# Block norms of a two-layer decoder trunk: from one root per token, spread by a diagonal product, to a ones product and roots on all partitions

## The chip, the cores and the metric

The kernel runs on one core of one Trainium2 chip. The metric is device time in microseconds for one execution of the whole program. A profiled execution leaves a trace besides; its span runs from the first to the last instruction that the profiler recorded.

## What is computed

The reference is a trunk of two layers over 512 tokens plus 16 meta tokens (528 columns here), with a model width of 1024. Everything is float32. Each layer is a feed-forward block, a token mixer and a second feed-forward block. The mixer of layer 0 is gated linear attention (GLA), that of layer 1 sliding-window attention over keys and values that are made once, after layer 0. Each of the six sub-layers has a norm on its input and a norm on its output:

```python
def rmsnorm(x, g):
    xf = x.astype(jnp.float32)
    y = xf * lax.rsqrt(jnp.mean(xf * xf, axis=-1, keepdims=True) + EPS)
    return (y * g.astype(jnp.float32)).astype(x.dtype)

h = h + 0.5 * rmsnorm(swiglu(rmsnorm(h, g[0]), w_ffn_in[layer, 0], w_ffn_out[layer, 0]), g[1])
...
h = h + rmsnorm(mix, g[3])
h = h + 0.5 * rmsnorm(swiglu(rmsnorm(h, g[4]), w_ffn_in[layer, 1], w_ffn_out[layer, 1]), g[5])
```

The mean runs over the 1024 features of a token. GLA has one more norm per head, over 256 features.

## The kernel before, in words

**Layout.** Features lie on the 128 partitions and tokens along the columns: H (the residual stream) and Y (a block's output) are tiles of 128 x 8 x 528. A norm therefore needs a sum across partitions, and its result, one number per token, is needed on every partition. Tokens come in two groups, columns 0 to 271 and 272 to 527 in layer 0 (`L0`), 16 to 271 and 272 to 527 in layer 1 (`L1`).

**Products.** TensorE (PE) multiplies in a split form. Each weight tile and each operand is kept as a high part, rounded by ScalarE (ACT), and a low part, the remainder that VectorE (DVE) makes by a subtraction; three products make one (`mm3`). Weights come by DMA into raw tiles and are split by `split_part` (L228, L229) or, for Strassen products, by `split_pair` (L248, L249; POOL issues the adding DMAs of L254). All products have the line of the helper `mm`, L164, so they are told apart by the names of their tiles.

**Norms.** `square_into` (L402, L405, L406) squares on ACT and sums six of eight feature tiles on GpSimd (POOL); first and last tile keep a buffer of their own (`acc`, six buffers), so a norm's sums are two tiles of 128 x n. A post-norm is `Residual.run`: `rstd` makes the roots, then for each of eight feature tiles DVE multiplies Y by them (L467) and adds to H (L468), `Operand.build` makes the next block's operand x from H (ACT L428 and DVE L429), and `sumsq` squares it for the pre-norm. The last post-norm, `Residual.store`, multiplies two feature tiles at a time (L482), adds (L483, partly on POOL) and sends the output (L485). A pre-norm is `Operand.factors`: x goes into its products without the root, and the root row R scales the products when they leave PSUM (L643, L647, L843 and others), so those evacuations wait for the job `rjob` of their group.

**rstd.** For c tokens at a time (128, or 68 for 272 columns) a product with a single column of ones puts the sums of c tokens into one column of the PSUM tile `st` (L357). The result has tokens on partitions: 128 x 2 or 68 x 4 numbers. A magic constant and two refining steps give the inverse root, ten small operations on DVE (post-norms and the two norms at the opening) or eleven on POOL behind one on ACT (L366). Then a diagonal matrix `dg` (L386) times ones, the tile `r`, spreads the roots over all partitions (L394). For post-norms r stays in PSUM and is read there; for pre-norms ACT copies it into R (L445).

**Order of the work.** All engines take their instructions in program order, and that order is planned when the program is written. `Flow` keeps a clock that PE's products advance, and every generator yields planned microseconds: `DCHAIN` (3.0) between st and r where the roots are made on DVE, `CHAIN` (5) where POOL makes them, 1.0 after each feature tile. A step that has come due is put into the queues at PE's next product. PSUM has eight banks (`ps`). At a block's end, `out_steps` finishes the first group's tiles, spawns its `Residual.run`, and multiplies the second group's tiles meanwhile; `x_first` then multiplies the next block's first four weight tiles for the first group, while the second group's post-norm runs, and then for the second group.

Of the kernel before, what the change touches and what calls it, by code (L numbers as in the profile page):

```python
# [11 lines left out]
I32 = mybir.dt.int32  # L12
AF = mybir.ActivationFunctionType
ALU = mybir.AluOpType
AX = mybir.AxisListType

P = 128
D = 1024
# [9 lines left out]
RSQRT_MAGIC = float(0x5F3759DF)  # L28
# [9 lines left out]
CHAINS = 2  # L38

CHAIN = 5  # L40
DCHAIN = 3.0
FACT = 1.5
START = 1.0
SECOND = 6.0
# [81 lines left out]
def trunk_kernel(ctx: ExitStack, tc, a, out):  # L126
    nc = tc.nc
    pe, act, dve, pool, sp = nc.tensor, nc.scalar, nc.vector, nc.gpsimd, nc.sync
# [11 lines left out]
    ident = cp.tile([P, P], F32, name="ident")  # L140
    hident = cp.tile([P, P], F32, name="hident")
    ones = cp.tile([P, P], F32, name="ones")
    eps = cp.tile([P, 1], F32, name="eps")
    zeros = cp.tile([P, P], F32R, name="zeros")

    def ps(name):
        return pp.tile([P, 512], F32, tag="ps", name=name)

    def pair_tile(name, dt=F32R):
        return hp.tile([P, 2, TOK], dt, tag="pair", name=name)  # L150
# [5 lines left out]
    def flat(t):  # L156
        return t.rearrange("p a t -> p (a t)")

    def gain(layer, i, k):
        c = V_GAIN + layer * 48 + i * 8 + k  # L160
        return vec[:, c : c + 1]

    def mm(o, lhs, rhs, start=True, stop=True, onto=False):
        inst = pe.matmul(o, lhs, rhs, start=start, stop=stop, skip_group_check=onto)  # L164
        n = 1
        for d in rhs.shape[1:]:
            n *= d
        flow.clock += n / 2400 if rhs.dtype == F32R else max(n / 600, 0.12)
        return inst
# [178 lines left out]
        mm3s([(o, w)], j, x, g, start, stop)  # L348


    def rstd(sq, n, dim, half, name, eng=pool):
        c = 128 if n % 128 == 0 else n // 4
        nch = n // c
        st = ps(f"st_{name}")
        for j in range(nch):
            for i, t in enumerate(sq):
                mm(st[:c, j : j + 1], t[:, j * c : (j + 1) * c], ones[:, 0:1], i == 0, i == len(sq) - 1)  # L357
        av = sm.tile([P, 4], F32, tag="av", name=f"av_{name}")
        yv = sm.tile([P, 4], F32, tag="yv", name=f"yv_{name}")
        zv = sm.tile([P, 4], F32, tag="zv", name=f"zv_{name}")  # L360
        wv = sm.tile([P, 4], F32, tag="wv", name=f"wv_{name}")
        aa, yy, zz, ww = av[:c, :nch], yv[:c, :nch], zv[:c, :nch], wv[:c, :nch]
        if eng is dve:
            dve.tensor_scalar(aa, st[:c, :nch], 1.0 / dim, 1e-6, op0=ALU.mult, op1=ALU.add)
        else:
            act.activation(aa, st[:c, :nch], AF.Identity, scale=1.0 / dim, bias=eps[:c])  # L366
        eng.tensor_scalar(yy.bitcast(I32), aa.bitcast(I32), -0.5, RSQRT_MAGIC, op0=ALU.mult, op1=ALU.add)

        eng.tensor_tensor(zz, yy, yy, op=ALU.mult)
        eng.tensor_tensor(zz, zz, aa, op=ALU.mult)  # L370
        eng.tensor_scalar(ww, zz, 0.375, -1.25, op0=ALU.mult, op1=ALU.add)
        eng.tensor_tensor(ww, ww, zz, op=ALU.mult)
        if eng is dve:
            dve.scalar_tensor_tensor(yy, ww, 1.875, yy, op0=ALU.add, op1=ALU.mult)
            dve.tensor_tensor(zz, yy, yy, op=ALU.mult)
            dve.scalar_tensor_tensor(zz, zz, -0.5, aa, op0=ALU.mult, op1=ALU.mult)
            dve.scalar_tensor_tensor(yy, zz, 1.5, yy, op0=ALU.add, op1=ALU.mult)
        else:
            pool.tensor_scalar(ww, ww, 1.875, None, op0=ALU.add)
            pool.tensor_tensor(yy, yy, ww, op=ALU.mult)  # L380
            pool.tensor_tensor(zz, yy, yy, op=ALU.mult)
            pool.tensor_tensor(zz, zz, aa, op=ALU.mult)
            pool.tensor_scalar(zz, zz, -0.5, 1.5, op0=ALU.mult, op1=ALU.add)
            pool.tensor_tensor(yy, yy, zz, op=ALU.mult)
        dg = sm.tile([P, 272], F32, tag="dg", name=f"dg_{name}", bufs=2)
        eng.tensor_tensor(  # L386
            dg[:c, :n].rearrange("p (j c) -> p j c", c=c),
            (hident if half else ident)[:c, :c].unsqueeze(1).to_broadcast([c, nch, c]),
            yy.unsqueeze(2).to_broadcast([c, nch, c]),
            op=ALU.mult,  # L390
        )
        yield DCHAIN if eng is dve else CHAIN
        r = ps(f"r_{name}")
        mm(r[:, :n], ones[:c, :], dg[:c, :n])  # L394
        return r


    def square_into(sums, src, i, count, name):
# [14 lines left out]
    class Operand:  # L413


        def __init__(self, name, gv, groups, rt=None):
            self.name, self.gv, self.groups, self.tiles = name, gv, groups, [None] * KD
            self.ready = set()
            self.rt = rt
            self.rjob = [None] * len(groups)  # L420
            self.accs = [[] for _ in groups]
# [14 lines left out]
            o, n = self.groups[gi]  # L436
            square_into(self.accs[gi], H[:, k, o : o + n], k, KD, f"{self.name}_{o}_{k}")

        def factors(self, gi, eng=pool):
            if self.rt is None:  # L440
                self.rt = sm.tile([P, TOK], F32, tag="R", name=f"R_{self.name}", bufs=2)
            o, n = self.groups[gi]
            yield FACT
            r = yield from rstd(self.accs[gi], n, D, False, f"{self.name}_{o}", eng)
            act.activation(self.rt[:, o : o + n], r[:, :n], AF.Copy)  # L445

        def need(self, gi, k):
            flow.until(lambda: (gi, k) in self.ready)
# [1 line left out]

    class Residual:
        def __init__(self, name, layer, i, half, nxt=None):
            self.name, self.half, self.nxt = name, half, nxt
            self.gain = lambda m: gain(layer, i, m)

        def run(self, gi, g, sums):
            o, n = g
            nxt = self.nxt
            yield 1.8
            r = yield from rstd(sums, n, D, self.half, f"post_{self.name}{gi}", dve)  # L460
            if nxt is None:
                yield from self.store(gi, g, r)
                return
            for k in range(KD):
                h, y = H[:, k, o : o + n], Y[:, k, o : o + n]
                t = r[:, 256 : 256 + n] if n <= 256 else ps(f"t_{self.name}{gi}{k}")[:, :n]
                dve.tensor_tensor(t, y, r[:, :n], op=ALU.mult)  # L467
                dve.tensor_tensor(h, t, h, op=ALU.add)  # L468
                nxt.build(gi, k)
                nxt.sumsq(gi, k)  # L470
                yield 1.0
            nxt.rjob[gi] = flow.spawn(nxt.factors(gi))

        def store(self, gi, g, r):
            o, n = g
            rb = r[:, :n].unsqueeze(1).to_broadcast([P, 2, n])
            for k in range(0, KD, 2):
                h, y = H[:, k : k + 2, o : o + n], Y[:, k : k + 2, o : o + n]
                last = gi == 1 and k < 4
                t = flat(pair_tile(f"t_{self.name}{k}", F32))[:, :512] if last else ps(f"t_{self.name}{gi}{k}")  # L480
                t = t.rearrange("p (k n) -> p k n", n=n)
                dve.tensor_tensor(t, y, rb, op=ALU.mult)  # L482
                (pool if last else dve).tensor_tensor(h, t, h, op=ALU.add)  # L483
                for j in (k, k + 1):
                    sp.dma_start(out[j, :, o - META : o - META + n], H[:, j, o : o + n])  # L485
                yield 1.0
# [330 lines left out]
    def gla(x, finish):  # L817
        set_ahead(10)
        with tc.tile_pool(name="gp", bufs=1) as gp:
# [61 lines left out]
            def core(h, before):  # L881
# [73 lines left out]
                s = flat(pair_tile(f"st{h}", F32))[:, :1024].rearrange("p (b v) -> p b v", v=256)  # L955
# [12 lines left out]
                for i in range(2):  # L968
                    vs = slice(i * P, (i + 1) * P)
                    p = ps(f"po{h}_{i}")  # L970
                    for b in range(4):
                        o = p[:, b * P : (b + 1) * P]
# [5 lines left out]
                yy = Y[:, 2 * h : 2 * h + 2]  # L978
                dve.tensor_copy(yy[:, :, :META], pm[:, : 2 * META].rearrange("p (i m) -> p i m", m=META))
                accs = []  # L980
# [3 lines left out]
                        square_into(accs[gi], Y[:, 2 * h + i, o : o + n], i, 2, f"go{h}_{gi}")  # L984
                yield 2.0
                def scale(gi, o, n):
                    r = yield from rstd(accs[gi], n, 256, True, f"go{h}_{gi}")
                    dve.tensor_tensor(
                        yy[:, :, o : o + n], yy[:, :, o : o + n],
                        r[:, :n].unsqueeze(1).to_broadcast([P, 2, n]), op=ALU.mult,  # L990
                    )
# [241 lines left out]
    x = Operand("l0f0", lambda k: gain(0, 0, k), L0)  # L1233
# [6 lines left out]
    def factors(gi):  # L1240
        for k in range(KD):
            x.sumsq(gi, k)
            yield 0.4
        yield START
        yield from x.factors(gi, dve)

    def second():
        for k in range(KD):
# [37 lines left out]
    nxt, fin = into("l0m", 0, 1, True, lambda k: gain(0, 2, k), L0)  # L1286
    ffn(x, L0, fin, True)
    x = nxt
    nxt, fin = into("l0f1", 0, 3, False, lambda k: gain(0, 4, k), L0)
    gla(x, fin)  # L1290
    x = nxt
    nxt, fin = into("kv", 0, 5, True, lambda k: vec[:, V_KVN + k : V_KVN + k + 1], L0)
# [3 lines left out]
    with tc.tile_pool(name="kp", bufs=1) as kp:  # L1296
        x = Operand("l1f0", lambda k: gain(1, 0, k), L1)
# [8 lines left out]
        nxt, fin = into("l1m", 1, 1, True, lambda k: gain(1, 2, k), L1)  # L1306
        ffn(x, L1W, fin)
        x = nxt
        nxt, fin = into("l1f1", 1, 3, False, lambda k: gain(1, 4, k), L1)
# [87 lines left out]
```

## Time and profile before

| | us |
|---|---|
| median of 3 runs | 1923.98 |
| lowest and highest | 1922.87, 1925.53 |
| the profiled execution | 1922.4 |
| its span | 1920.6 |
| PE busy in the span | 1885.4 |
| DVE, ACT, POOL busy | 1340.4, 993.5, 341.4 |

The profiled execution lies 1.6 us under the median. Busy times of engines overlap and don't add up. PE has two rows: PE for products and PEld for the loads of the stationary operand, which overlap with products. A row of a group gives line, engine, operation, tiles written and read, shapes, the count, busy us and the mean ns of one, and then the idle time before them with what ended it. A row in order of time begins with start and duration in us. In names such as `st_post_l0m` the last part is the block that comes next: l0f (twice: first and second feed-forward of layer 0), l0m (GLA), kv, l1f, l1m (attention), out.

### The profile page before, as it was taken

How to read it: one execution, taken by the hardware profiler on the slowest of the kernel's cores; microseconds unless marked ns; L12 is line 12 of the kernel's file. 1: busy time of each engine (PE TensorE's matmuls, PEld its weight loads, DVE VectorE, ACT ScalarE, POOL GpSimd, SP SyncE). 2: the span in 40 equal slices, each digit the busy share in tenths (PEclk: the TensorE clock that was granted, in tenths of full speed). 3: DMA queues.
4: the chain of work that ended last, by engine and by line, in shares of the span. 5: the costliest groups of instructions: out<-in, count | busy, mean ns of one | idle time of the engine just before them, and what ended most of it. 6: DMA issues, size and time to landing. Idle time of an engine off the chain costs nothing.

```text
span 1920.6 us, 37874 instructions
## 1 busy us (share of the span) xinstructions
PE 1885.4 (98%) x14522; PEld 1798.7 (94%) x14522; DVE 1340.4 (70%) x2724; ACT 993.5 (52%) x2268; POOL 341.4 (18%) x561
## 2 busy tenths in 40 slices
PE   8999999999999999999999999999998999999997
PEld 8999999999999999999999898989976898989897
DVE  7884848676364787475877775858688778758584
ACT  5662626553245556363674563636645665636363
POOL 2101010311111410101034011010351141010102
PEclk9999999999999999999999999999998999999998
DMA  5655556222113145556642356565321215565651
GB/s 180 149 154 142 153 142 171 98 78 74 38 56 111 57 121 149 149 149 149 161 159 56 96 148 157 144 159 165 111 67 34 69 50 126 148 152 157 152 144 45
DMA packets 133253, 231.29 MB, mean 120 GB/s; under 512 B 14928, under 2 KB 27728, under 8 KB 133072
## 3 DMA queue, kind: packets, MB, share of 16 engines
q1 hardware_dynamic: 112048, 190.99, 30.8%
q0 software_dynamic: 20736, 37.76, 12.6%
q8 instruction: 113, 1.85, 0.4%
q14 instruction: 68, 0.56, 0.1%
q10 hardware_dynamic: 288, 0.13, 0.0%
HBM read 226.72 MB, written 2.10 MB: 119 GB/s over the span
## 4 chain that ended last, share of the span: by engine, by line
PE 89%; DVE 6%; ACT 2%; POOL 1%; issue 1%; DMA 0%; SPq 0%; DVEq 0%; POOLq 0%; ACTq 0%
PE y L164 31%; PE a L164 21%; PE x L164 16%; PE c L164 9%; PE d L164 5%; PE o L164 1%; DVE w L229 1%; PE e L164 1%; PE po L164 1%; PE sc L164 1%; ACT w L228 1%; PE ps L164 0%; DVE x_l0f L429 0%; PE st_go L164 0%; DVE w_s L249 0%
## 5 line engine op out<-in xcount | busy, mean ns | idle before, releaser
L254 POOL DMA_DIRECT2D raw<-in_w_in x144 | 125.9, 935 | 968.2 <-DMA raw<-in_w_in 443.9
L249 DVE TENSOR_TENSOR w_s<-raw,w_s 128x512 fp32r<-128x512 f32 x288 | 194.8, 688 | 109.3 <-ACT w_s L248 107.6
L164 PE MATMUL y<-hidl0f,w 128*128 128x272 f32 (+1 forms) x2112 | 261.0, 285 | 0.0
L164 PEld LDWEIGHTS y<-hidl0f,w 128*128 128x128 f32 x2112 | 258.8, 188 | 0.2
L229 DVE TENSOR_TENSOR w<-raw,w 128x512 fp32r<-128x512 f32 x378 | 243.7, 672 | 21.0 <-ACT w L228 18.7
L164 PE MATMUL y<-hidl1f,w 128*128 128x512 f32 (+1 forms) x1344 | 249.4, 346 | 0.0
L164 PEld LDWEIGHTS y<-hidl1f,w 128*128 128x128 f32 x1344 | 212.3, 188 | 33.2 <-ACT hidl1f L410 0.5
L248 ACT ACTIVATE w_s<-raw 128x512 fp32r<-128x512 f32 x288 | 177.6, 625 | 108.8 <-DVE raw L264 69.1
L228 ACT ACTIVATE w<-raw 128x512 fp32r<-128x512 f32 x378 | 207.9, 587 | 35.0 <-PE y L164 26.9
L249 DVE TENSOR_TENSOR w<-raw,w 128x512 fp32r<-128x512 f32 x216 | 145.2, 687 | 37.6 <-ACT w L248 35.9
L164 PE MATMUL x<-x_l0m,w 128*128 128x272 f32 (+1 forms) x1200 | 158.3, 288 | 0.0
L248 ACT ACTIVATE w<-raw 128x512 fp32r<-128x512 f32 x216 | 130.4, 621 | 47.9 <-PE y L164 47.6
L164 PEld LDWEIGHTS x<-x_l0m,w 128*128 128x128 f32 x1200 | 149.4, 188 | 1.2
L590 DVE TENSOR_TENSOR Y<-y,Y 128x256 f32<-128x256 f32 (+2 forms) x176 | 82.1, 473 | 92.0 <-PE y L164 91.6
L164 PE MATMUL a<-zl0f_t,w_s 128*128 128x264 f32 x864 | 117.0, 285 | 0.0
L164 PE MATMUL a<-zl1f_t,w_s 128*128 128x256 f32 x864 | 114.2, 281 | 0.7 <-ACT c L783 0.6
L164 PEld LDWEIGHTS a<-zl0f_t,w_s 128*128 128x128 f32 x864 | 110.1, 188 | 0.0
L164 PEld LDWEIGHTS a<-zl1f_t,w_s 128*128 128x128 f32 x864 | 106.9, 188 | 1.8 <-ACT c L783 1.7
L406 POOL TENSOR_TENSOR acc_post<-acc_post,sq_post 128x256 f32<-128x256 f32 (+1 forms) x72 | 57.5, 799 | 281.2 <-ACT sq_post L405 280.8
L164 PE MATMUL x<-x_l0f,w 128*128 128x256 f32 (+1 forms) x768 | 99.6, 289 | 7.3 <-ACT w L228 5.8
L164 PEld LDWEIGHTS x<-x_l0f,w 128*128 128x128 f32 x768 | 96.3, 191 | 8.6 <-ACT w L228 5.8
L164 PE MATMUL x<-x_l1f,w 128*128 128x256 f32 (+1 forms) x576 | 92.9, 320 | 0.0
(487 smaller groups left out, 3411.0 us busy)
## 6 DMA issues: line engine op xcount, KB each, us to landing
raw<-in_w_in SPq DMA_DIRECT2D x424, 256.0 KB, 3.8
raw<-in_w_in POOLq DMA_DIRECT2D x144, 256.0 KB, 5.0
raw<-in_w_out SPq DMA_DIRECT2D x96, 256.0 KB, 3.5
raw<-in_gla_in SPq DMA_DIRECT2D x50, 256.0 KB, 3.2
raw<-in_w_last SPq DMA_DIRECT2D x48, 256.0 KB, 3.5
raw<-in_w_out SPq DMA_DIRECT2D x64, 128.0 KB, 3.0
raw<-in_gla_out SPq DMA_DIRECT2D x16, 256.0 KB, 2.8
raw<-in_w_q SPq DMA_DIRECT2D x16, 256.0 KB, 3.8
```

The lines of the kernel that those rows point to most:

```text
L164: inst = pe.matmul(o, lhs, rhs, start=start, stop=stop, skip_group_check=onto)
L228: act.activation(w[:, 0, :m], raw[:, :m], AF.Copy)
L229: dve.tensor_tensor(w[:, 1, :m], raw[:, :m], w[:, 0, :m].bitcast(F32), op=ALU.subtract)
L248: act.activation(w[:, 0, :512], src, AF.Copy)
L249: dve.tensor_tensor(w[:, 1, :512], src, w[:, 0, :512].bitcast(F32), op=ALU.subtract)
L254: pool.dma_start(dst, src, accum_op=ALU.add)
L406: pool.tensor_tensor(sums[0][:, :n], sums[0][:, :n], t[:, :n], op=ALU.add)
L590: dve.tensor_tensor(y, p[:, :n], y, op=ALU.add)
```

## The change

The norms of `Residual` and `Operand` no longer call `rstd`; it stays for GLA's head norms alone, on POOL. They call a new function, `roots`. It multiplies the two tiles of sums by the full 128 x 128 matrix of ones, which puts each token's sum on every partition (tile `st`, 128 x n in PSUM). One planned microsecond later (`SUMMED`, 1.0) it puts five operations into the queues: on ACT the table function Abs_reciprocal_sqrt and a Square of it, on DVE one Newton step in three operations. The result is written into SBUF: into the second tile of sums for a post-norm, into R for a pre-norm. There is no diagonal, no r, and no copy into R. In a post-norm with at most 256 columns the two halves of the bank `st` serve in turns as the scratch for Y times root.

```diff
-DCHAIN = 3.0
+SUMMED = 1.0
...
+    def roots(sums, n, c, name, dst=None):
+        s = ps(f"st_{name}")
+        for i, t in enumerate(sums):
+            mm(s[:, :n], ones, t[:, :n], i == 0, i == len(sums) - 1)
+        yield SUMMED
+        q, y = sums[0][:, :n], sums[1][:, :n] if dst is None else dst
+        act.activation(y, s[:, :n], AF.Abs_reciprocal_sqrt, scale=1.0 / D, bias=eps)
+        act.activation(q, y, AF.Square, scale=D ** -0.5)
+        dve.scalar_tensor_tensor(q, s[:, :n], D * 1e-6, q, op0=ALU.add, op1=ALU.mult)
+        dve.tensor_scalar(q, q, -0.5 * c, 1.5 * c, op0=ALU.mult, op1=ALU.add)
+        dve.tensor_tensor(y, q, y, op=ALU.mult)
+        return y, s
...
-        def factors(self, gi, eng=pool):
+        def factors(self, gi):
...
             yield FACT
-            r = yield from rstd(self.accs[gi], n, D, False, f"{self.name}_{o}", eng)
-            act.activation(self.rt[:, o : o + n], r[:, :n], AF.Copy)
+            yield from roots(self.accs[gi], n, 1.0, f"{self.name}_{o}", self.rt[:, o : o + n])
...
-            r = yield from rstd(sums, n, D, self.half, f"post_{self.name}{gi}", dve)
+            r, s = yield from roots(sums, n, self.c, f"post_{self.name}{gi}")
...
-                t = r[:, 256 : 256 + n] if n <= 256 else ps(f"t_{self.name}{gi}{k}")[:, :n]
-                dve.tensor_tensor(t, y, r[:, :n], op=ALU.mult)
+                c = k % 2 * 256
+                t = s[:, c : c + n] if n <= 256 else ps(f"t_{self.name}{gi}{k}")[:, :n]
+                dve.tensor_tensor(t, y, r, op=ALU.mult)
...
-            rb = r[:, :n].unsqueeze(1).to_broadcast([P, 2, n])
+            rb = r.unsqueeze(1).to_broadcast([P, 2, n])
...
-        yield from x.factors(gi, dve)
+        yield from x.factors(gi)
```

More of the change, by code (lines that the diff above doesn't have):

```diff
@@ L348, in mm3, with rstd @@
         mm3s([(o, w)], j, x, g, start, stop)
-    def rstd(sq, n, dim, half, name, eng=pool):
+    def rstd(sq, n, dim, name):
         c = 128 if n % 128 == 0 else n // 4
@@ L362, in rstd @@
         aa, yy, zz, ww = av[:c, :nch], yv[:c, :nch], zv[:c, :nch], wv[:c, :nch]
[L363 to L384, printed above, removed]
+        act.activation(aa, st[:c, :nch], AF.Identity, scale=1.0 / dim, bias=eps[:c])
@@ new lines, in rstd @@
+        pool.tensor_scalar(yy.bitcast(I32), aa.bitcast(I32), -0.5, RSQRT_MAGIC, op0=ALU.mult, op1=ALU.add)
+        pool.tensor_tensor(zz, yy, yy, op=ALU.mult)
+        pool.tensor_tensor(zz, zz, aa, op=ALU.mult)
+        pool.tensor_scalar(ww, zz, 0.375, -1.25, op0=ALU.mult, op1=ALU.add)
+        pool.tensor_tensor(ww, ww, zz, op=ALU.mult)
+        pool.tensor_scalar(ww, ww, 1.875, None, op0=ALU.add)
+        pool.tensor_tensor(yy, yy, ww, op=ALU.mult)
+        pool.tensor_tensor(zz, yy, yy, op=ALU.mult)
@@ L385, in rstd @@
+        pool.tensor_tensor(zz, zz, aa, op=ALU.mult)
+        pool.tensor_scalar(zz, zz, -0.5, 1.5, op0=ALU.mult, op1=ALU.add)
+        pool.tensor_tensor(yy, yy, zz, op=ALU.mult)
         dg = sm.tile([P, 272], F32, tag="dg", name=f"dg_{name}", bufs=2)
-        eng.tensor_tensor(
+        pool.tensor_tensor(
             dg[:c, :n].rearrange("p (j c) -> p j c", c=c),
-            (hident if half else ident)[:c, :c].unsqueeze(1).to_broadcast([c, nch, c]),
+            hident[:c, :c].unsqueeze(1).to_broadcast([c, nch, c]),
@@ L391, in rstd @@
         )
-        yield DCHAIN if eng is dve else CHAIN
+        yield CHAIN
         r = ps(f"r_{name}")
@@ L452, in __init__ @@
         def __init__(self, name, layer, i, half, nxt=None):
-            self.name, self.half, self.nxt = name, half, nxt
+            self.name, self.c, self.nxt = name, 0.5 if half else 1.0, nxt
             self.gain = lambda m: gain(layer, i, m)
@@ L986, in scale @@
                 def scale(gi, o, n):
-                    r = yield from rstd(accs[gi], n, 256, True, f"go{h}_{gi}")
+                    r = yield from rstd(accs[gi], n, 256, f"go{h}_{gi}")
                     dve.tensor_tensor(
```

## The prediction

> **What bounds the kernel now.** I read the page first, then busy time by stages, then TensorE's weight loads in order of time, then its waits. The page's first lines:
>
> ```profile
> span 1920.6 us, 37874 instructions
> PE 1885.4 (98%) x14522; PEld 1798.7 (94%) x14522; DVE 1340.4 (70%) x2724; ACT 993.5 (52%) x2268; POOL 341.4 (18%) x561
> PE 89%; DVE 6%; ACT 2%; POOL 1%; issue 1%; DMA 0%; SPq 0%; DVEq 0%; POOLq 0%; ACTq 0%
> ```
>
> TensorE (PE) is busy for 98% of the span and carries 89% of the chain that ended last. A share over the whole span can hide the stages where block norms sit, so the next view cuts those out: stage, its length, then PE, PEld, DVE, ACT, POOL busy us.
>
> ```profile
> 345.00:425.00 80.00, 80.00 (x657) 79.09 (x656) 50.01 (x127) 45.34 (x99) 26.38 (x53) 1.00 0.20 65
> 610.00:690.00 80.00, 78.77 (x653) 78.00 (x653) 56.59 (x133) 41.80 (x98) 23.83 (x45) 1.00 0.17 47
> 980.00:1060.00 80.00, 78.43 (x646) 76.97 (x645) 59.09 (x154) 41.15 (x97) 32.64 (x55) 1.00 0.21 61
> 1360.00:1430.00 70.00, 67.61 (x504) 61.85 (x502) 47.98 (x127) 33.76 (x85) 39.04 (x64) 1.00 0.13 41
> 1535.00:1595.00 60.00, 59.95 (x435) 56.22 (x434) 46.94 (x118) 35.60 (x83) 26.39 (x48) 1.00 0.21 58
> 1906.30:1920.60 14.30, 2.18 (x10) 1.32 (x9) 6.15 (x18) 0.92 (x2) 2.48 (x2) 0.65 0.22 73
> ```
>
> The first five are the boundaries between sub-layers, where a post-norm (Residual) and the next pre-norm (Operand.factors) lie. PE idles there for 0, 1.2, 1.6, 2.4 and 0.05 us, 5.2 us in all. So even there PE is the bound: an instruction taken off PE is worth its own time, and a shorter chain on another engine is worth almost nothing, except in the last line, the 14.3 us after the last block product, where PE is nearly empty and latency counts in full.
>
> **The change, part by part.** It touches 24 norms: 6 Residuals and 6 Operands with two token groups each. Seven of these groups have 272 columns (the first group of three Residuals and of four Operands), 17 have 256. The eight head norms of GLA keep rstd.
>
> *TensorE.* Before, a norm puts sums into columns (st) and later spreads the roots with one product (r). PE's weight loads around one boundary, start and length:
>
> ```profile
> 378.69 1.13 PEld L164 LDWEIGHTS st_l0m<-ones,acc_l0m 128*68 128x68 f32 x16
> 379.74 0.97 PEld L164 LDWEIGHTS st_post_l0m<-ones,acc_post 128*128 128x128 f32 x8
> 380.63 4.33 PEld L164 LDWEIGHTS x<-x_l0m,w 128*128 128x128 f32 x34
> 384.90 0.31 PEld L164 LDWEIGHTS r_post_l0m<-dg_post_l0m,ones 128*128 128x128 f32 x2
> 385.24 0.53 PEld L164 LDWEIGHTS x<-x_l0m,w 128*128 128x128 f32 x3
> 385.71 0.32 PEld L164 LDWEIGHTS r_l0m<-dg_l0m,ones 68*128 68x128 f32 x2
> 386.06 4.67 PEld L164 LDWEIGHTS x<-x_l0m,w 128*128 128x128 f32 x36
> ```
>
> The cost of a group is from its start to the next row's start. st costs 1.05 us for 272 columns (16 instructions) and 0.89 for 256 (8 instructions, a single output column each); r costs 0.35 and 0.34. An f32 product is two instructions in the trace. After, a norm is two products ones x sums, each with the stationary operand, width and type of r, so 2 x 0.34 or 2 x 0.35. Per norm of 256: 0.89 + 0.34 - 0.68 = 0.55 us less. Per norm of 272: 1.05 + 0.35 - 0.70 = 0.70 less. 17 x 0.55 + 7 x 0.70 = **14.3 us less PE work**, all in stages where PE is the bound. What is late next there are the weights and x tiles behind PE; the five stages' 5.2 us of idle PE say that both mostly keep up now.
>
> *Waits of PE.* From PE's waits (us in total, times, longest):
>
> ```profile
> PE r_post_out L164 <- DVE dg_post_out L386: 2.6, 1, 2.6
> PE st_l1m L164 <- POOL acc_l1m L406: 1.1, 1, 1.1
> PE st_l0f L164 <- ACT acc_l0f L402: 1.1, 1, 1.1
> PE r_post_kv L164 <- DVE dg_post_kv L386: 0.7, 1, 0.7
> PE st_kv L164 <- POOL acc_kv L406: 0.6, 1, 0.6
> PE r_l0f L164 <- DVE dg_l0f L386: 0.5, 1, 0.5
> PE r_kv L164 <- POOL dg_kv L386: 0.2, 1, 0.2
> PE r_l0f L164 <- POOL dg_l0f L386: 0.2, 1, 0.2
> ```
>
> The product r goes away, and with it the only place where PE waits for the roots: 0.7 + 0.5 + 0.2 + 0.2 = **1.6 us less** (the 2.6 is in the tail, below). The waits of st for its sums stay, now before the ones product; I count them unchanged.
>
> *The chain of one norm.* The post-norm of the same boundary's second group, on DVE:
>
> ```profile
> 380.84 0.16 DVE L364 TENSOR_SCALAR av_post_l0m<-st_post_l0m 128x2 f32<-128x2 f32 x1 [3.14 <-PE st_post_l0m L164]
> 382.82 0.42 DVE L386 TENSOR_TENSOR dg_post_l0m<-hident,yv_post_l0m 128x256 f32<-128x256 f32 x1
> 385.65 0.43 DVE L467 TENSOR_TENSOR r_post_l0m<-Y,r_post_l0m 128x256 f32<-128x256 f32 x1 [2.41 <-PE r_post_l0m L164]
> ```
>
> From st to the first multiply it is 385.65 - 379.74 = 5.9 us; 1.7 of them pass between the diagonal's end (383.24) and r's turn in PE's queue (384.90), an order fixed by the planner's yield. The new operations have no row of their own, so they are bounded by these:
>
> ```profile
> L867 ACT ACTIVATE az<-z,vec 128x272 f32<-128x272 f32 (+1 forms) x8 | 3.3, 488 | 4.1 <-PE z L164 4.1
> L868 DVE TENSOR_SCALAR ls<-z,vec 128x256 f32<-128x256 f32 x4 | 1.9, 478 | 0.0
> L371 DVE TENSOR_SCALAR wv_post_l1m<-zv_post_l1m 128x2 f32<-128x2 f32 x2 | 0.3, 170 | 0.1
> ```
>
> The root is an ACTIVATE from PSUM with a bias pointer, as L867: 0.49. Square: 0.41, as the first row of the three under the table loads below. The three DVE operations on 128x256 lie between 0.17 (the same kind on two columns) and 0.48; I take 0.43 for each, as the diagonal and the multiply above take 0.42 and 0.43. From r's weight load to the reader is 385.65 - 384.90 = 0.75. New chain: 0.34 + 0.75 + 0.49 + 0.41 + 3 x 0.43 + some 0.15 of handoffs = 3.4 us, 2.5 shorter. By the bounds it is 2.6 to 3.6. In these stages that buys nothing by itself; it is slack.
>
> *Load on the other engines.* DVE: 14 old chains (12 post, two at the opening) of ten small operations in 2.0 us (380.84 to 382.82) and a diagonal of 0.42, 34 us, against 24 x 1.29 = 31. POOL loses ten chains. ACT gains 24 x (0.49 + 0.41) = 22 us, less the ten small av rows and twelve R copies that go, **and table loads**.
>
> *Table loads.* All of them today, and one in order of time:
>
> ```profile
> L644 ACT ACT_TABLE_LOAD x3 | 3.8, 1283 | 0.1
> L1231 ACT ACT_TABLE_LOAD x1 | 1.3, 1283 | 1.2 <-PEq L1386 1.2
> L872 ACT ACT_TABLE_LOAD x1 | 1.3, 1283 | 0.0
> L905 ACT ACT_TABLE_LOAD x1 | 1.3, 1283 | 0.0
> L1162 ACT ACT_TABLE_LOAD x1 | 1.3, 1283 | 0.7 <-DVE nm L1158 0.7
> ```
> ```profile
> 1570.40 0.41 ACT L405 ACTIVATE sq_l1f<-H 128x256 f32<-128x256 f32 x1
> 1570.83 1.28 ACT L644 ACT_TABLE_LOAD   x1
> 1572.12 0.42 ACT L644 ACTIVATE gu<-gu 128x256 f32<-128x256 f32 x1
> ```
>
> Seven loads: Silu, Ln and Exp need theirs; Copy, Square and Identity need none. I assume the root needs a table apart from Silu's and Exp's. By the order of the code that gives, beyond the seven: opening 3, into GLA 2 (root, then Tanh again), into the second FFN 3, shared KV 2, attention 1, last FFN 3, end 1: 15 more, 15 x 1.283 = 19.2 us of ACT. If it shares Silu's table it is almost none. ACT is busy 45 of 80, 42 of 80, 41 of 80, 34 of 70 and 36 of 60 us in the five stages, so 1.3 to 3.8 us more fits. Most lie off the path of the x tiles: the root's first load comes while PE multiplies the second token group of the block before; Silu's load among the second group's x tiles is there already (1570.83); and the reloads for the second pre-norm come when all x tiles of that norm are built. Their cover is the x products that PE has queued; without it each costs 1.28.
>
> [...]
>
> *Queues.* All five operations of a norm are put into ACT's and DVE's queues 1.0 us of planned time after the products. DVE's three wait at the queue's head for ACT's two (0.9 us, 2.2 with a load). Behind them on DVE stand the block's evacuations (L590), weight splits (L229) and the multiplies of the other group; for those wait PE's banks and x tiles. The second group's x tiles are the tight spot. I charge **2 us more** over the kernel, between -3 (the shorter chain and a POOL free for the L406 sums take away idle PE) and +31 (second rival).
>
> *The tail.* From the last sum to the last multiply:
>
> ```profile
> 1907.26 0.74 PEld L164 LDWEIGHTS st_post_out<-ones,acc_post 128*128 128x128 f32 x6 [0.89 <-ACT acc_post L402]
> 1912.04 2.49 DVE L482 TENSOR_TENSOR t_out<-Y,r_post_out 128x512 f32<-128x512 f32 x4 [1.45 <-PE r_post_out L164]
> ```
>
> After: 1907.26 + 0.75 (second product) + 0.49 + 0.41 + 1.29 + 0.15 = 1910.4, no load among them, as the first group has already fetched the table. That is **1.6 us less**.
>
> **Sum.** -14.3 - 1.6 - 1.6 + 2 = -15.5. The profiled execution took 1922.4 us (span 1920.6 and 1.8 around it), so 1906.9. The median of the runs, 1923.98, is 1.6 above that execution; on its scale the forecast is 1908.
>
> **The rivals.**
> (1) *More is won.* The shorter chain and the free POOL also remove idle PE at the boundaries and the st waits of 1.1, 1.1 and 0.6: about 5 us more, with 2 us not charged, 1902. For it: the second group's x tiles start 2.5 us earlier. Against: their pace is set by DVE's work per tile, which stays.
> (2) *Slower: PE waits for x tiles because DVE stands behind ACT.* Place: the second group at each boundary. Price if nothing is hidden: 24 x 0.9 of DVE standing and 15 x 1.28 of loads, 41 us, less about 2 us of slack at each of five boundaries, 31: 1922.4 - 17.5 + 31 = 1936. It decides once about 17 of the 41 reach PE. For it: DVE is 63 to 78% busy there (50 of 80 to 47 of 60). Against: the old chain held PE back 1.7 us in its queue and the new one doesn't. [...]
> (3) *Partly hidden.* Half of the loads beside x tiles show, some 8 us: 1916.
> (4) *The ones product is no cheaper* than st and r together: then only waits and tail remain, -3.2 + 2, 1922 to 1923. The row of r, same operands and width, speaks against it.
>
> **How the numbers follow.** Forecast 0.58 (1905 to 1912), (1) 0.14, (3) 0.12, (2) 0.10, (4) 0.06. The range is 1899 to 1921. A difference of 0.2% (3.9 us) is about what a measurement can tell from none. Forecast, (1) and (3) are faster: 0.84; (4) is mostly no difference, 0.06; (2) slower, 0.10.
>
> **What would show it.** Right: PE's busy time falls by some 14 us; no rows r_post or R copies; st rows of four instructions with about 0.7 us to the next row; 22 table loads or so; t_out starts 3.1 us after the last sum. Wrong: new PE waits for x tiles or w in the five stages, ends of DVE waits on the root's line over 2 us, or s products that cost over 0.5 us each.

## The result, and the profile after

The changed kernel takes 1935.34 us (median of 6 runs, 1931.64 to 1937.82) against 1922.98 (6 runs, 1922.22 to 1925.53): ratio **1.0055, interval 1.0044 to 1.0066**, so slower by half a per cent. The forecast was 1908. The page after, the lines that answer to the three shown of before:

```profile
span 1934.6 us, 37301 instructions
PE 1883.9 (97%) x14322; PEld 1794.5 (93%) x14322; DVE 1357.9 (70%) x2642; ACT 1026.4 (53%) x2309; POOL 316.1 (16%) x441
...
PE 84%; DVE 9%; ACT 4%; issue 1%; POOL 1%; DMA 0%; SPq 0%; DVEq 0%; ACTq 0%; POOLq 0%
```

PE has 200 instructions fewer, yet is busy only 1.5 us less, and the span is 14.0 us longer. So PE's idle time grew by 15.5 us, and its remaining work became longer. DVE and ACT hold 13% of the chain that ended last, where they held 8%. The boundaries, stage by stage as before (each shifted by the time already lost, the last two 2 us longer):

```profile
345.00:425.00 80.00, 77.20 (x585) 75.14 (x584) 49.21 (x106) 46.53 (x97) 21.92 (x29) 0.96 0.15 50
615.00:695.00 80.00, 77.69 (x618) 76.17 (x618) 61.44 (x126) 49.06 (x108) 18.61 (x21) 1.00 0.16 47
985.00:1065.00 80.00, 73.54 (x577) 71.55 (x576) 59.69 (x136) 44.13 (x98) 25.96 (x31) 0.98 0.20 56
1368.00:1440.00 72.00, 67.39 (x479) 60.66 (x479) 53.45 (x125) 37.92 (x93) 35.29 (x40) 0.98 0.13 45
1548.00:1610.00 62.00, 58.45 (x401) 54.35 (x399) 50.35 (x109) 40.31 (x88) 18.97 (x23) 0.97 0.17 48
```

PE now idles 2.8, 2.3, 6.5, 4.6 and 3.6 us there, 19.7 in all where it was 5.2, and its granted clock (the third number from the end) is below 1 in four of the five. What it waits for, in the view of PE's waits (us in total, times, longest), behind a first row of 5.7 us at the opening that was there before (5.8):

```profile
PE ptm L176 <- DVE mt L1175: 5.1, 2, 2.9
PE st_kv L164 <- POOL acc_kv L411: 4.8, 2, 3.1
PE st_l1m L164 <- POOL acc_l1m L411: 3.9, 2, 2.6
PE pk L176 <- DVE f L920: 3.3, 1, 3.3
PE st_l1f L164 <- POOL acc_l1f L411: 2.0, 1, 2.0
PE st_l0m L164 <- POOL acc_l0m L411: 2.0, 1, 2.0
PE o L164 <- DVE pt L1196: 1.8, 1, 1.8
PE st_kv L164 <- ACT acc_kv L407: 1.6, 2, 1.0
```

The st rows are the ones products of pre-norms, which stand in PE's queue before their sums of squares are there. All st waits but the tail's come to 18.7 us (1.5 of them at a post-norm), against 2.8 before. That growth of 15.9 us is as large as all of PE's new idle time. The other waits change too, but nearly cancel: those for r are gone (4.2 us with the tail's), and so are those for sc in attention (6.7), while those for ptm, pk and o, steps of attention and GLA, grow by 8.2. In order of time at the boundary that the prediction showed (weight loads):

```profile
375.26 0.30 PEld L164 LDWEIGHTS st_l0m<-acc_l0m,ones 128*128 128x128 f32 x2 [2.18 <-POOL acc_l0m L411]
376.98 0.50 PEld L164 LDWEIGHTS st_l0m<-acc_l0m,ones 128*128 128x128 f32 x2 [1.42 <-ACT acc_l0m L407]
377.60 6.53 PEld L164 LDWEIGHTS x<-x_l0m,w 128*128 128x128 f32 x33
384.07 0.75 PEld L164 LDWEIGHTS st_post_l0m<-acc_post,ones 128*128 128x128 f32 x4
384.85 8.04 PEld L164 LDWEIGHTS x<-x_l0m,w 128*128 128x128 f32 x63
```

Two waits of 2.18 and 1.42 us, one for each tile of sums. Then 33 loads of x products take 6.5 us, where 63 take 8.0 a little later: 0.20 us apiece against 0.13. The clock says why:

```profile
376.00:380.00 4.00, 3.18 (x12) 2.79 (x12) 1.63 (x5) 3.28 (x8) 1.28 (x3) 0.50 0.00 0
380.00:384.00 4.00, 4.00 (x25) 4.00 (x24) 0.72 (x2) 0.00 (x0) 0.00 (x0) 0.69 0.00 0
384.00:390.00 6.00, 6.00 (x47) 5.90 (x47) 3.52 (x10) 2.34 (x6) 0.00 (x0) 1.00 0.02 4
```

From 376 to 380 PE is granted half its clock, in the next 4 us 0.69 of it: by single microseconds 0.50 from 376 to 382, 0.74 in the next, 1.00 from 383. Waits of 3.6 us by the weight loads thus cost about 6. The rows show this fall after these two waits; how long a wait brings it was not shown.

Why the sums are late is in the chain of the post-norm ahead of it. DVE and ACT for the first group before kv, from product to first multiply:

```profile
990.38 0.76 PEld L164 LDWEIGHTS st_post_kv<-acc_post,ones 128*128 128x128 f32 x4
...
991.78 1.28 ACT L395 ACT_TABLE_LOAD   x1
993.07 0.49 ACT L395 ACTIVATE acc_post<-st_post_kv,eps 128x272 f32<-128x272 f32 x1
...
993.46 0.62 ACT L228 ACTIVATE w<-raw 128x512 fp32r<-128x512 f32 x1
...
994.38 0.42 ACT L396 ACTIVATE acc_post<-acc_post 128x272 f32<-128x272 f32 x1
...
995.31 0.78 DVE L398 TENSOR_SCALAR acc_post<-acc_post 128x272 f32<-128x272 f32 x1
...
996.60 0.80 DVE L472 TENSOR_TENSOR t_kv<-Y,acc_post 128x272 f32<-128x272 f32 x2
```

That is 6.2 us from 990.38 to 996.60: the load, ACT's other work between root and Square (a weight split and a gain), and a DVE operation of 0.78. Of the six first groups four take 5.2 to 5.5 us, this one 6.2, and the one before the second feed-forward 4.1, where the load ran ahead of the product. The old chain took as long (986.93 to 993.29 in the trace of before), but the plan gave it 3.0 us and gives the new one 1.0. And many of the multiplies that follow are slower. They read two operands from SBUF now, Y and the root row; psumroot and nopool below test whether that is why. DVE's groups by form:

```profile
L472 DVE TENSOR_TENSOR st_post_l1m<-Y,acc_post 128x256 f32<-128x256 f32 x16 | 8.7, 544 | 0.2
...
L472 DVE TENSOR_TENSOR t_kv<-Y,acc_post 128x272 f32<-128x272 f32 x8 | 5.0, 638 | 0.0
```

The same multiplies took 422 and 436 ns with the root row in PSUM. Over all 80 of them DVE is busy 44.4 us instead of 34. One that is slow, beside POOL's row:

```profile
1002.14 1.71 POOL L411 TENSOR_TENSOR acc_kv<-acc_kv,sq_kv 128x272 f32<-128x272 f32 x2 [0.54 <-ACT sq_kv L410]
```
```profile
1002.19 1.03 DVE L472 TENSOR_TENSOR t_kv<-Y,acc_post 128x272 f32<-128x272 f32 x1
```

The tail shows it at its largest:

```profile
1922.10 0.30 PEld L164 LDWEIGHTS st_post_out<-acc_post,ones 128*128 128x128 f32 x2 [0.88 <-ACT acc_post L407]
...
1925.10 4.64 DVE L487 TENSOR_TENSOR t_out<-Y,acc_post 128x512 f32<-128x512 f32 x4
1925.87 3.31 POOL L488 TENSOR_TENSOR H<-t_out,H 128x512 f32<-128x512 f32 x2 [5.00 <-DVE t_out L487]
```

The multiply starts 3.0 us after the last product's load, as forecast (3.1), but the four take 4.64 us instead of 2.49, and POOL's two adds 3.31 instead of 2.48. Counted to the end of the multiplies, the tail gains 1.8 and gives 2.2 back. The span's end, behind the output's DMA, still comes 12.5 us after that load, where it came 13.3.

### The profile page after: what moved, and what is told of

Its sections match the earlier page's. It is cut to its first block, busy times and chain, and to the rows that moved or that the text cites. A ratio compares the mean times of both kernels' runs of the same rounds, so it can differ in the third digit from the quotient of the medians.

```text
span 1934.6 us, 37301 instructions
## 1 busy us (share of the span) xinstructions
PE 1883.9 (97%) x14322; PEld 1794.5 (93%) x14322; DVE 1357.9 (70%) x2642; ACT 1026.4 (53%) x2309; POOL 316.1 (16%) x441
## 4 chain that ended last, share of the span: by engine, by line
PE 84%; DVE 9%; ACT 4%; issue 1%; POOL 1%; DMA 0%; SPq 0%; DVEq 0%; ACTq 0%; POOLq 0%
PE y L164 28%; PE a L164 20%; PE x L164 15%; PE c L164 9%; PE d L164 5%; PE o L164 1%; DVE H L473 1%; DVE w L229 1%; PE e L164 1%; PE po L164 1%; ACT w L228 1%; PE sc L164 0%; PE ps L164 0%; DVE x_kv L434 0%; DVE x_l1f L434 0%
## 5 line engine op out<-in xcount | busy, mean ns | idle before, releaser
L164 PE MATMUL y<-hidl0f,w 128*128 128x256 f32 (+1 forms) x2112 | 260.3, 285 | 0.0
L164 PE MATMUL x<-x_l0m,w 128*128 128x256 f32 (+1 forms) x1200 | 160.8, 292 | 0.0
```

## The experiments

Three theories: **P**, the planned delay of 1.0 us is too short, and PE runs into its own queue; **S**, the root row in SBUF slows DVE while POOL works; **L**, the table loads on ACT set the pace. Each ratio is to the kernel before, measured again beside that run (its median there is 1924.5 to 1925.3), so differences between runs are taken from the ratios.

**plan4**

```diff
-SUMMED = 1.0
+SUMMED = 4.0
```

> The changed kernel with the planned delay between the ones product and the root's five operations set to 4.0 us instead of 1.0; nothing else. Theory P (the plan is short: the post-norm's real chain from product to first multiply takes 5.2 to 6.2 us for the first group against 1.0 planned, so the pre-norm's ones product stands in PE's queue before its sums, PE waits some 19 us there against 4 before, and its clock falls to half after such waits): PE's waits on st fall under 6 us and the time to about 1912 (1905 to 1918). Theory L (the 16 more table loads on ACT set the pace): no less than 1930. Theory S (the root row now lies in SBUF, so the multiply L472 reads two SBUF operands and slows from 0.43 to 0.54 to 0.64 us while POOL works, 10 us in all on DVE): no less than 1928.

Measured 1915.27 us, ratio 0.9952 (0.9940 to 0.9965). As P has it in time: one constant of the plan is worth 20 us. The st waits fall to 7.7 us and not under 6. The constant also delays the pre-norms' roots, and the waits for ptm, pk and o fall with it, from 10.2 to 2.9 us; P says nothing of that, and psum_post4 below takes the two apart. (The number of loads in the text on record is one too high: the trace has 22, 15 more than before.)

**noload**

```diff
-        act.activation(y, s[:, :n], AF.Abs_reciprocal_sqrt, scale=1.0 / D, bias=eps)
+        act.activation(y, s[:, :n], AF.Identity, scale=1.0 / D, bias=eps)
...
-        dve.tensor_scalar(q, q, -0.5 * c, 1.5 * c, op0=ALU.mult, op1=ALU.add)
-        dve.tensor_tensor(y, q, y, op=ALU.mult)
+        dve.tensor_scalar(q, q, 0.0, c, op0=ALU.mult, op1=ALU.add)
+        dve.scalar_tensor_tensor(y, y, 0.0, q, op0=ALU.mult, op1=ALU.add)
```

> The changed kernel with Identity in the place of the root's table function and constants in the Newton step, so that every norm factor is a constant: the same instructions on the same engines, but no table loads beyond those of before. Leaves out the norms' values. Theory L: 16 loads of 1.28 us go, the time falls by some 19 to about 1916. Theory P: the chain is 1.3 us shorter where a load stood in it, and the waits shrink by that in perhaps six of the ten places: 1926 to 1932. Theory S: 1933 to 1936.

Measured 1929.14 us, ratio 1.0026 (1.0015 to 1.0036), about 6 us less than with the loads. L's 19 us are refuted; the 6 are what P allows them as parts of a chain that PE waits for.

**psumroot**

```diff
-        dve.tensor_tensor(y, q, y, op=ALU.mult)
-        return y, s
+        z = s[:, :n] if dst is None else y
+        dve.tensor_tensor(z, q, y, op=ALU.mult)
+        return z, s
...
-                c = k % 2 * 256
-                t = s[:, c : c + n] if n <= 256 else ps(f"t_{self.name}{gi}{k}")[:, :n]
+                t = s[:, 256 : 256 + n] if n <= 256 else ps(f"t_{self.name}{gi}{k}")[:, :n]
```

> The changed kernel with the post-norm's root row written into the PSUM bank of the sums instead of the SBUF tile; the scratch for Y times root is the other half of that bank, as before the change. Same count of instructions. Theory S: L472 returns to 0.43 us, t_out in the tail from 1.16 to 0.69 us, and the time falls by 10 or more, to 1918 to 1925. Theory P: the tail gives back some 2 us and each group's x tiles come about 1 us earlier, so 1928 to 1932. Theory L: 1932 to 1935.

Measured 1916.84 us, ratio 0.9959 (0.9945 to 0.9972): 18 us for the place of one row of roots, and 1 us below the range of S. L472 is back where it was:

```profile
L472 DVE TENSOR_TENSOR st_post_l1m<-Y,st_post_l1m 128x256 f32<-128x256 f32 x16 | 6.8, 423 | 0.2
```

The st waits fall to 9.6 us, since the x tiles and squares behind each multiply come earlier.

**psum4**, both edits.

> Both edits: planned delay 4.0 and the root row in PSUM. If P and S are the causes together: the 14 us of PE work show at last, with 3 us in the tail: 1904 to 1912. Theory L: no less than 1928.

Measured **1900.43 us, ratio 0.9876 (0.9862 to 0.9889)**, faster than both kernels, by 24 and 34 us, and 3.6 us below the expected range. Its page, PE's only st waits, and two of the boundaries:

```profile
span 1900.1 us, 37301 instructions
PE 1872.4 (99%) x14322; PEld 1786.0 (94%) x14322; DVE 1337.3 (70%) x2642; ACT 1024.3 (54%) x2309; POOL 310.0 (16%) x441
```
```profile
PE st_post_out L164 <- ACT acc_post L408: 0.5, 1, 0.5
PE st_l0f L164 <- ACT acc_l0f L408: 0.5, 1, 0.5
```
```profile
345.00:425.00 80.00, 80.00 (x633) 78.84 (x633) 52.02 (x115) 50.96 (x104) 20.86 (x29) 1.00 0.20 60
...
980.00:1060.00 80.00, 80.00 (x609) 77.11 (x608) 60.22 (x148) 43.70 (x99) 23.27 (x29) 1.00 0.17 47
```

PE is busy throughout these two boundaries at full clock, and its busy time in the span is 13.0 us below that of before: the saving that the prediction counted shows once PE isn't made to wait. The other 7.5 us of the 20.5 by which this span is shorter than that of before are idle time of PE. Against the changed kernel the span falls by 34.5 us, of which 11.5 are PE's busy time (the same 14322 instructions at a mean granted clock of 0.996 instead of 0.989) and 23.0 its idle time.

**psum_post4**

```diff
-        yield SUMMED
+        yield 1.0 if dst is not None else SUMMED
```

> psum4 with the planned delay of 4.0 kept for post-norms and 1.0 for pre-norms. Theory P1 (what counts is where the post-norm's delay puts the next pre-norm's ones product in PE's queue): no st wait comes back, 1899 to 1903. Rival P2 (what counts is the pre-norm's own delay, which puts the evacuations and Silu behind it too early into the queues of DVE and ACT): half or more of the 16 us between psumroot and psum4 is lost, 1909 to 1917.

Measured 1905.59 us, ratio 0.9899 (0.9886 to 0.9913), 4 to 5 above psum4. Between the two, nearer to P1: of the 16 us from psumroot to psum4 the post-norm's delay brings some 11 and takes the st waits away but for 0.5 us. The rest goes with the pre-norm's delay, by the order in attention and GLA: PE's waits for ptm are 5.3 us against 1.6 in psum4, for pk 3.3 against 1.3, for o 1.8 against none.

**psum4_noload**, psum4 with the edit of noload.

> psum4 with Identity in the place of the table function and constants in the Newton step: no table loads beyond those of before; leaves out the norms' values. The 15 loads (22 against 7, 19 us of ACT) are covered now that no st wait is left: 1897 to 1901, at most 3 us below psum4. Rival (loads still show): 1885 to 1893.

Measured 1898.92 us, ratio 0.9867 (0.9852 to 0.9882). That is 1.5 us under psum4 by the medians, and the intervals overlap: once the waits are gone, no cost of the loads can be told from none.

**nopool**

```diff
-        pool.tensor_tensor(sums[0][:, :n], sums[0][:, :n], t[:, :n], op=ALU.add)
```

> The changed kernel, root row in SBUF and delay 1.0, without POOL's sums of squares (L411); leaves out six of the eight feature tiles of every block norm's sums. Theory S1 (L472 with two SBUF operands is slow only while POOL works on SBUF): all L472 at 0.42 to 0.45 us, none above 0.5, t_out in the tail still slowed by POOL's own adds. Rival S2 (two SBUF operands are slower in themselves, or by ACT): means stay at 0.50 to 0.64. In time: the st waits on POOL's sums go too, so 1912 to 1922 under S1, 1922 to 1930 under S2.

Measured 1909.91 us, ratio 0.9926 (0.9912 to 0.9939), a little faster than S1 had it. Two of the groups (L471 here), which took 638 and 578 ns in the changed kernel:

```profile
L471 DVE TENSOR_TENSOR t_kv<-Y,acc_post 128x272 f32<-128x272 f32 x8 | 3.5, 444 | 0.0
...
L471 DVE TENSOR_TENSOR st_post_kv<-Y,acc_post 128x256 f32<-128x256 f32 x8 | 4.0, 502 | 0.1
```

Six of the eight groups stand at 0.43 to 0.44 us with both operands still in SBUF. In the other two the means are 457 (st_post_l1m) and 502 ns (st_post_kv), so "none above 0.5" did not hold; POOL's rotary products are left here, and in the changed kernel a multiply of st_post_kv beside one of them (L1042, 0.95 us from 1031.62) took 1.00 us. t_out in the tail, beside POOL's adds, is as slow as ever (958 ns in the mean, 957 in the changed kernel, 688 before). So it is POOL's work, not the place of the operand alone, nor ACT. (The time says less: the st waits fall to 4.5 us here too, as the sums no longer wait for POOL.) POOL's work alone doesn't do it either: before, with the root row in PSUM, a multiply of t_kv at 998.94 beside two adds of squares (1.72 us from 998.89) took 0.44 us, and none of the 80 more than 0.45; the one shown above, with both operands in SBUF, took 1.03. How POOL's work holds the multiply up was not shown. The TENSOR_SCALAR of the chain, with one input, is slowed as well; its shortest, median and longest ns in the changed kernel and here:

```profile
L398 DVE TENSOR_SCALAR acc_post<-acc_post x12: 293/296/789, 361.7 to 1924.3; 128x256 f32<-128x256 f32 x9, 128x272 f32<-128x272 f32 x3
```
```profile
L398 DVE TENSOR_SCALAR acc_post<-acc_post x12: 293/295/302, 360.7 to 1897.4; 128x256 f32<-128x256 f32 x9, 128x272 f32<-128x272 f32 x3
```

**psum4_twice**

```diff
-        for i, t in enumerate(sums):
-            mm(s[:, :n], ones, t[:, :n], i == 0, i == len(sums) - 1)
+        for i, t in enumerate(sums * 2):
+            pe.matmul(s[:, :n], ones, t[:, :n], start=i % 2 == 0, stop=i % 2 == 1)
+        flow.clock += n / 300
```

> psum4 with every ones product made twice (48 more products of 0.34 to 0.38 us on PE, the same sums). If PE work at the boundaries is worth its own time, as the prediction's 14 us took it: 24 x 0.70 = 17 us more than psum4, 1914 to 1919. Rival (PE has slack there and the gain of psum4 is from somewhere else): 1900 to 1906.

Measured 1919.24 us, ratio 0.9970 (0.9959 to 0.9982): 18 us more by the ratios, for 48 products, 0.38 us each. PE work at the boundaries is worth its own time.

**psum2h**, psum4 with `SUMMED = 2.5`.

> psum4 with the planned delay 2.5 instead of 4.0 (root row in PSUM). Theory P: the real chain of the first group is some 5 us from product to multiply with 0.7 of products planned besides, so at 2.5 some of the st waits are back: 1903 to 1912, between 1916.8 at 1.0 and 1900.4 at 4.0. Rival (only 4.0 happens to give a good order): 1913 to 1918.

Measured 1908.02 us, ratio 0.9907 (0.9895 to 0.9920), inside P's range, but only in part for P's reason. PE's waits, the first rows after the opening's:

```profile
PE ptm L176 <- DVE mt L1175: 5.1, 2, 2.9
PE pk L176 <- DVE f L920: 3.3, 1, 3.3
PE o L164 <- DVE pt L1196: 1.7, 1, 1.7
```

The st waits that are back come to 1.3 us; these three come to 10.1, as in psum_post4, and to 2.9 in psum4. So from 1.0 to 2.5 (psumroot to this run) the st waits fall by 8 us and the time by 10, and from 2.5 to 4.0 the waits in attention and GLA fall by 7 and the time by 6.

**psum5h**, psum4 with `SUMMED = 5.5`.

> psum4 with the planned delay 5.5. Theory P: PE no longer waits at st already at 4.0, so more delay buys nothing and puts x tiles and evacuations later: 1900 to 1906. Rival (the chain is still under-planned): 1896 to 1899.

Measured 1918.92 us, ratio 0.9968 (0.9956 to 0.9980): missed by 13 us. PE has no st waits there either but the tail's 0.5, and waits 5.2 us for GLA's diagonals (r_go, 1.7 in psum4), 3.8 for ptm (1.6), and 1.9 for x tiles of attention (none). So P explains why too short is bad, not how bad too long is. That a late pre-norm reorders the attention and GLA steps is read from these waits and was not tried by itself.

**before_plan4**

```diff
-DCHAIN = 3.0
+DCHAIN = 4.0
```

> The kernel before with its planned delay for DVE's roots at 4.0 instead of 3.0. Its PE waits on st and r were 3.6 and 1.6 us; if those go, 1920 to 1922; if r's later place costs as much, 1923 to 1926. Rival to the whole reading (the old kernel was short of planned delay too, and psum4's gain is the plan's alone): 1905 to 1912.

Measured 1930.18 us, ratio 1.0024 (1.0014 to 1.0034): a miss on the slow side, with PE's waits for ptm at 4.9 us, 0.7 before. This longer delay alone does not give the old kernel psum4's gain; no other delay was tried there, nor one of its pre-norms (`CHAIN`).

## Why the prediction was wrong, step by step

**PE work, -14.3.** Right in kind, some 2 us too large. In psum4 a norm's products take about 0.81 us (272 columns) and 0.78 (256) from first load to the next row, where 0.70 and 0.68 were counted; against st and r of before that saves about 12 us. PE is busy 13.0 us less there (at a mean granted clock of 0.996, before 0.995), and the time grows by 18 us when the products are doubled. The gain was lost to the waits and to the clock, which fell after them (mean 0.989 in the changed kernel) and hid it in the busy time of the changed kernel.

**"The waits of st for its sums stay; I count them unchanged."** This is the step that failed first: 2.8 us became 18.7, and more through the clock. The prediction names the planned 1.0 us but doesn't follow it to the next ones product, which moves up by 2.0 us in PE's queue, while the first group's chain, which its sums wait for, did not get shorter where a load stood in it. With the post-norms' delay alone at 4.0 (psum_post4) 0.5 us of these waits is left. The pre-norms' planned delay fell too, from 5 where POOL made the roots to 1.0; the prediction doesn't price that, and by psum_post4 it is worth 4 to 5 us.

**The chain, 3.4 us (2.6 to 3.6).** For three of the five second groups ahead of the tail it holds (384.07 to 387.52, 3.5 us); the others take 3.9 and 4.8. For five of the six first groups it is 5.2 to 6.2: the term left out the load, which I had priced and called covered, and the other work in ACT's queue between root and Square.

**The multiply from SBUF.** Its cost was taken as nothing without a word: the root row moved from PSUM to SBUF, and 0.43 us became 0.51 to 0.64. By psumroot that is 18 us, the mis-sized term next to the plan. In the tail it took the gain back by the end of the multiplies.

**Table loads.** 22 as counted, 1.283 us each, and followed at once by the next activation (991.78 + 1.28 to 993.07). Not to be told from none in psum4; some 6 us in the changed kernel.

**The 2 us for queues, and the rivals.** Rival (2) named the second group's x tiles and DVE behind ACT, and gave 1936. The time is near, but not for that cause: what PE waited for was mostly the sums at its own early product, and removing the loads removed 6 us, not its 19.

## What to carry to other kernels

When a step gets a shorter planned delay, compare the delay with its real latency in each place, queue by queue: here TensorE paid 18.7 us for products that stood in its queue ahead of their sums, and again in clock, at 0.50 after such a wait. A planned delay also places what comes later: of the 16 us between delays of 1.0 and 4.0, some 10 went with the waits for sums, some 6 with steps of attention and GLA. Moving an operand from PSUM to SBUF can slow a VectorE operation beside GpSimd, here at 272 columns from 0.44 to 1.03 us at the worst; price it from a row that has GpSimd busy beside it. After a change, first see whether the saving that was counted is there under the new waits; here it was, and two small edits brought it out.

## What the runs showed that was not expected

With the root row in PSUM, one constant moves this kernel by 16 to 18 us in both directions: 1916.8, 1908.0, 1900.4 and 1918.9 us at delays of 1.0, 2.5, 4.0 and 5.5. Two waits of 3.6 us in all were followed by a granted clock of 0.50 for some 6 us. A TENSOR_SCALAR of 128x256 in SBUF takes 0.29 us, two thirds of a TENSOR_TENSOR of that size (0.43), but 0.78 where POOL was adding squares; without those sums (nopool) the longest of the twelve post-norms' takes 302 ns. Code that the change did not touch is slow too where the new order puts it beside POOL, here in attention:

```profile
1447.01 1.33 POOL L1043 TENSOR_TENSOR q<-q,sh_q 128x512 f32<-128x512 f32 x1 [0.94 <-DVE den L1173]
```
```profile
1447.13 1.76 DVE L1176 TENSOR_TENSOR Y<-Y,den 128x512 f32<-128x512 f32 x1
```

Before, that operation on Y took 0.69 us at most. What this costs in time was not tried.
